# The low parts of five weight tiles computed on GpSimd instead of VectorE, in a hybrid decoder layer on one core

## The chip, the cores and the metric

One core of a Trainium2 chip runs the whole kernel. The metric is the time of one execution on the device, in microseconds (us); smaller is better. Engines are named as the profile names them: PE (TensorE), ACT (ScalarE), DVE (VectorE), POOL (GpSimd), SP (SyncE, which here only issues DMAs).

## The reference, cut to what matters

One decoder layer on 512 positions of width 1024: a mixer of three parallel branches, cross-attention to 256 memory rows, and a gated MLP. The change lies in the mixer, whose input product `h @ w_in` feeds every branch:

```python
xa, ga, q, k, v, z, beta_raw, alpha_raw, uc, gates = jnp.split(h @ w_in, offs, axis=-1)
ya = rg_lru(causal_dwconv(xa, a_conv_w) + a_conv_b, a_w_r, a_b_r, a_w_i, a_b_i, a_lam) * jax.nn.gelu(ga)
...
o = chunk_gated_delta_rule(q, k, v, g, beta)
...
yc = jax.nn.gelu(s5_layer(uc, c_lam_re, c_lam_im, c_log_dt, c_b_re, c_b_im, c_c_re, c_c_im, c_d))
yc = (yc * jax.nn.sigmoid(yc @ c_glu_w.astype(f32) + c_glu_b.astype(f32))).astype(h.dtype)
branches = jnp.stack([ya, yb, yc], axis=2)
proj = jnp.einsum('bskc,kcd->bskd', branches, w_branch)
gate = jax.nn.sigmoid((gates + b_gate).reshape(bsz, s, N_BRANCH, D_MODEL))
return jnp.sum(gate * proj, axis=2) @ w_out
```

`rg_lru` takes two sigmoids of small block products of `xa`, forms `a = exp(log_a)` and `b = sqrt(1 - a*a) * ig * x`, and runs the recurrence `h = a*h + b` along the sequence. `s5_layer` runs a complex recurrence with 64 states in each of 32 groups.

## The kernel before, in words

**Weights.** All weights come as 179 tiles of 128 x 1024 (512 KB), in the order of the list `ORDER` (L40). Each product is float32 made of three passes of a rounded form: a weight tile `raw` is loaded by SP (`w_dma`, L207), ACT copies it rounded into `whi` (`w_split`, L222, by `act` at L145), and `wlo = raw - whi` is one `tensor_tensor` of 128 x 1024 (L223, by `tt` at L148; on DVE). PE then multiplies, for each of 8 slabs of 128 rows, `whi` by the high part of the activations, `whi` by their low part, and `wlo` by their high part (`passes`, L235): 24 products of 128 x 512 for a tile, the third of which is the first to read `wlo`. The names in the profile are `hh` and `hl` for the activations' two parts, `ps_in` and `ps_gate` for the results.

**Buffers.** `raw`, `whi` and `wlo` have three buffers each (`WB` = 3), so `whi` of tile n is written into the buffer of tile n-3, and waits until PE has done with that tile. `wnext` (L227) splits two tiles ahead.

**The stretch around the change.** Tiles 17 to 30 in `ORDER` are: 17 `("in", XA)`, 18 `("in", GA)`, 19 and 20 the second pair of `XA`, `GA`, 21 to 24 the four `Z_` tiles, 25 to 28 the last two pairs of `XA`, `GA`, 29 to 32 `gate` tiles of the first branch, and after these `("br", 0, 0)`, the first branch's products. Beside these products run three generators, each of which hands out its small work a piece at a time between the weight products: `rglru` (L900, four calls: PE makes `pr` and `pi` from `xfga`, ACT takes tanh, exp and a square root, DVE the `MEMSET` of one column at L921, the scan at L924 and the split into `yah` and `yal`), the gated delta rule (transposes `trp` on PE, whose squares ACT sums into `ss` through `junk`), and `s5` (L1085). In `s5`, ACT copies `ks` from the products `pk` (L1171), SP writes it to DRAM as `kd` with eight DMAs (L1176), and eight DMAs on ACT's queue read it back into `T` (L1194), which POOL has cleared before (L815). DVE meanwhile forms `F` from `fa`, `fb`, turns `rot` by two doublings (`s5_double`, L1068), and then does four rounds of a rotation into `Wd`, two scans `ra` (L1215) and a rotation back; for each round POOL makes a small tensor `D` (a `MEMSET` of 128 x 4 and one operation of 128 x 252). POOL's other work ahead of it is the polynomial of the gates' exponentials (`ge`, `gr`, from L822) and the first doublings of `rot` (L809).

**Order.** The program is written in the order of the generators, but the framework's scheduler (`schedule_with_timeline_sim=True`) sorts each engine's instructions by a simulated timeline; an engine then runs its own list strictly in that order, and its DMA queue likewise.

Of the kernel before, what the change touches and what calls it, by code (L numbers as in the profile page):

```python
# [10 lines left out]
ALU = mybir.AluOpType  # L11
# [25 lines left out]
XA, GA, Q_, K_, V_, Z_ = 0, 4, 8, 12, 16, 20  # L37


def weight_order():  # L40
    o = [("uc", t) for t in range(4)]
    for b in (K_, Q_, V_):
        o += [("in", b + t) for t in range(4)]
        if b == Q_:
            o.insert(-3, ("ba",))
    for t in range(4):
        o += [("in", XA + t), ("in", GA + t)]
        if t == 1:
            o += [("in", Z_ + t) for t in range(4)]
    for br in (0, 2, 1):  # L50
        gt = lambda mp: [("gate", br * 8 + 2 * mp), ("gate", br * 8 + 2 * mp + 1)]
        ahead = GA_N[br]
        first = [k for mp in range(ahead) for k in gt(mp)]
        if br == 1:
            for m in range(2):
                o += [("wk", 4 * m + i) for i in range(4)] + [("gate", br * 8 + m)]
            for c in range(2):
                o += [("wv", c, kp) for kp in range(4)] + [("gate", br * 8 + 2 + c)]
        else:
            o += first  # L60
        if br == 2:
            o += [("glu", 0), ("glu", 1)]
        for mp in range(4):
            o += (gt(mp) if mp >= ahead else []) + [("br", br, mp)]
    o += [("out", m) for m in range(8)]
    o += [("wq", m) for m in range(8)]
    o += [("wo", m) for m in range(8)]
    for half in range(2):
        for i in range(12 * half, 12 * half + 12):
            o += [("up", i), ("up", 24 + i)]  # L70
        if half == 0:
            o += [("down", c, kp) for c in range(2) for kp in range(6)]
        else:
            o += [("dn9", t) for t in range(9)] + [("dn3", t) for t in range(3)]
    return o


ORDER = weight_order()


class Layout:
# [20 lines left out]
class Kern:  # L102
# [104 lines left out]
    def w_dma(self, upto):  # L207
        while self.dma_i < min(upto, len(ORDER)):
            i = self.dma_i
            t = self.raw.tile([128, 1024], F32, tag="raw", name=f"raw{i}")  # L210
            self.nc.sync.dma_start(out=t, in_=self.ap["wts"][i])
            self.rawt[i] = t
            self.dma_i += 1

    def w_split(self, upto):
        while self.split_i < min(upto, len(ORDER)):
            i = self.split_i
            self.w_dma(i + 1)
            r = self.rawt.pop(i)
            h = self.whi.tile([128, 1024], F32R, tag="hi", name=f"whi{i}")  # L220
            l = self.wlo.tile([128, 1024], F32R, tag="lo", name=f"wlo{i}")
            self.act(h, r)  # L222
            self.tt(l, r, h, ALU.subtract)  # L223
            self.wt[i] = (h, l)
            self.split_i += 1

    def wnext(self, key, ahead=WB - 1):  # L227
        i = self.wi
        assert ORDER[i] == key, (ORDER[i], key)
        self.wi += 1  # L230
# [577 lines left out]
    def gt(self, out, a, b, op):  # L808
        return self.pin(self.nc.gpsimd.tensor_tensor(out=out, in0=a, in1=b, op=op))  # L809
# [745 lines left out]
def tiles_of(inputs):  # L1555
# [6 lines left out]

    out = np.empty((len(ORDER), 128, 1024), np.float32)
    for i, key in enumerate(ORDER):
        t, o = key[0], out[i]
# [119 lines left out]
```

## Time and profile before

| what | value |
|---|---|
| median of three runs | 1071.02 us (1071.0 to 1071.41) |
| the profiled execution | 1071.09 us |
| its span in the profile | 1069.2 us |
| granted TensorE clock, mean | 0.998 of full speed |
| PE busy | 1050.0 us, 98% of the span |
| DVE busy | 700.9 us, 66% |
| ACT busy | 502.7 us, 47% |
| POOL busy | 148.8 us, 14% |

The span runs from the first recorded instruction to the last; the 1.9 us between it and the execution's time lie outside the records. Times within the span are counted from its start. Shares are means over stages that are limited by different things, so a stage is read by its own rows.

### The profile page before, as it was taken

The page shows a single profiled execution, that of the slowest core. Times are in us where ns is not written, and L with a number is a line of the kernel's source. Part 1 is how long each engine was busy: PE and PEld are TensorE (multiplying, and loading weights), DVE is VectorE, ACT ScalarE, POOL GpSimd, SP SyncE. Part 2 cuts the span into 40 slices and gives each one's busy share as a digit, 9 for nine tenths or more (in the row PEclk, how much of TensorE's full clock was granted, in tenths as well). Part 3 has the DMA queues.
Part 4 walks back from the last instruction along what each step waited for, and adds up shares of the span by engine and source line. Part 5 has one row for each costly group of instructions (what it writes and reads, how often), then busy time and mean ns, then how long its engine had stood idle before and what let it go on. Part 6 is the DMA issues. An engine that isn't in the chain of part 4 may idle for free.

```text
span 1069.2 us, 13413 instructions
## 1 busy us (share of the span) xinstructions
PE 1050.0 (98%) x5098; PEld 873.9 (82%) x5098; DVE 700.9 (66%) x1024; ACT 502.7 (47%) x808; POOL 148.8 (14%) x285
## 2 busy tenths in 40 slices
PE   8999999999999999999999999999999999999996
PEld 6878878788877898888888878888888888888885
DVE  6798589958899554755545456577763357777423
ACT  6566766658244444633444344544442124444313
POOL 6899822000000100000000000000000000000004
PEclk9999999999999999999999999999999999999999
DMA  8362232255324431432422114222223233222222
GB/s 288 118 158 80 67 100 79 80 126 189 109 79 148 109 100 64 145 125 96 145 100 95 59 37 139 81 99 99 80 98 99 99 99 99 99 98 91 91 75 79
DMA packets 45168, 112.81 MB, mean 106 GB/s; under 512 B 10656, under 2 KB 16432, under 8 KB 44848
## 3 DMA queue, kind: packets, MB, share of 16 engines
q1 hardware_dynamic: 41088, 108.52, 31.7%
q10 hardware_dynamic: 3760, 3.18, 1.0%
q0 software_dynamic: 256, 0.26, 0.3%
q8 instruction: 40, 0.66, 0.3%
q14 instruction: 24, 0.20, 0.1%
HBM read 107.08 MB, written 4.86 MB: 105 GB/s over the span
## 4 chain that ended last, share of the span: by engine, by line
PE 67%; DVE 13%; POOL 12%; issue 3%; ACT 2%; DMA 1%; SPq 0%; POOLq 0%; ACTq 0%; DVEq 0%
PE ps_up L160 24%; PE psdn L160 11%; PE ps_gate L160 6%; PE ps_wq L160 4%; PE ps_out L160 4%; PE ps_wo L160 4%; POOL s5p L809 3%; PE psb L160 3%; DVE wlo L148 2%; PE ps_wk L160 2%; PE psv L160 2%; POOL s5P L153 2%; DVE nBX L148 1%; POOL s5p L154 1%; PE sc L160 1%
## 5 line engine op out<-in xcount | busy, mean ns | idle before, releaser
L148 DVE TENSOR_TENSOR wlo<-raw,whi 128x1024 fp32r<-128x1024 f32 (+1 forms) x185 | 220.2, 1194 | 168.8 <-ACT whi L145 163.8
L145 ACT ACTIVATE whi<-raw 128x1024 fp32r<-128x1024 f32 (+1 forms) x185 | 189.9, 1030 | 285.2 <-PE psdn L160 84.1
L160 PE MATMUL ps_up<-xgh,whi 128*128 128x512 f32 x384 | 150.2, 391 | 0.0
L160 PE MATMUL ps_up<-xgh,wlo 128*128 128x512 f32 x384 | 150.0, 391 | 0.0
L160 PE MATMUL ps_up<-xgl,whi 128*128 128x512 f32 x384 | 149.5, 389 | 0.0
L148 POOL TENSOR_TENSOR y<-xt,gfin 128x512 f32<-128x512 f32 x4 | 5.4, 1343 | 688.9 <-DVE xt L148 688.9
L160 PEld LDWEIGHTS ps_up<-xgh,wlo 128*128 128x128 f32 x384 | 72.1, 188 | 15.4 <-issue 0.2
L160 PEld LDWEIGHTS ps_up<-xgh,whi 128*128 128x128 f32 x384 | 72.1, 188 | 14.9 <-issue 0.2
L160 PEld LDWEIGHTS ps_up<-xgl,whi 128*128 128x128 f32 x384 | 72.1, 188 | 14.7
L160 PE MATMUL ps_gate<-hh,whi 128*128 128x512 f32 x192 | 75.6, 394 | 1.5 <-DVE pr L157 1.5
L160 PE MATMUL ps_gate<-hh,wlo 128*128 128x512 f32 x192 | 75.4, 393 | 0.0
L160 PE MATMUL ps_gate<-hl,whi 128*128 128x512 f32 x192 | 75.1, 391 | 0.0
L160 PE MATMUL psdn<-wlo,acth 128*128 128x512 f32 x192 | 74.4, 389 | 0.0
L160 PE MATMUL psdn<-whi,actl 128*128 128x512 f32 x192 | 74.4, 389 | 0.0
L160 PE MATMUL psdn<-whi,acth 128*128 128x512 f32 x192 | 73.9, 389 | 0.0
L157 DVE SCALAR_TENSOR_TENSOR fu<-pad,par,fu 128x512 f32<-128x512 f32 x96 | 71.5, 749 | 1.8 <-ACT fu L145 0.3
L160 PE MATMUL ps_in<-hh,whi 128*128 128x512 f32 x168 | 67.8, 403 | 0.0
L160 PE MATMUL ps_in<-hh,wlo 128*128 128x512 f32 x168 | 65.8, 392 | 0.1
L160 PE MATMUL ps_in<-hl,whi 128*128 128x512 f32 x168 | 65.7, 391 | 0.0
L148 DVE TENSOR_TENSOR pad<-ps_up,rb 128x512 f32<-128x512 f32 x48 | 32.9, 688 | 44.8 <-PE ps_up L160 43.5
L145 ACT ACT_TABLE_LOAD x32 | 41.1, 1283 | 18.8 <-DVE yp L157 10.1
L160 PEld LDWEIGHTS ps_gate<-hh,whi 128*128 128x128 f32 x192 | 36.1, 188 | 9.3 <-DVE pr L157 1.9
(394 smaller groups left out, 2181.8 us busy)
## 6 DMA issues: line engine op xcount, KB each, us to landing
raw<-wts SPq DMA_DIRECT2D x177, 512.0 KB, 3.4
x<-xT SPq DMA_DIRECT2D x14, 256.0 KB, 4.2
raw<-wts SPq DMA_DIRECT2D x8, 128.0 KB, 4.8
BC<-bc SPq DMA_DIRECT2D x1, 1024.0 KB, 8.2
ud<-uperm SPq DMA_DIRECT2D x4, 256.0 KB, 3.2
U<-ud SPq DMA_DIRECT2D x8, 128.0 KB, 6.2
uu<-ud SPq DMA_DIRECT2D x4, 256.0 KB, 3.4
yd<-T SPq DMA_DIRECT2D x8, 128.0 KB, 3.2
```

The lines of the kernel that those rows point to most:

```text
L145: return self.nc.scalar.activation(out=out, in_=in_, func=func, **k)
L148: return (eng or self.nc.vector).tensor_tensor(out=out, in0=a, in1=b, op=op)
L153: return e.tensor_scalar(out=out, in0=a, scalar1=s1, scalar2=None, op0=op0)
L154: return e.tensor_scalar(out=out, in0=a, scalar1=s1, scalar2=s2, op0=op0, op1=op1)
L157: return self.nc.vector.scalar_tensor_tensor(out=out, in0=a, scalar=s, in1=b, op0=op0, op1=op1)
L160: return self.nc.tensor.matmul(out, lhsT=lhsT, rhs=rhs, start=start, stop=stop)
L809: return self.pin(self.nc.gpsimd.tensor_tensor(out=out, in0=a, in1=b, op=op))
```

## The change

A constant names every third weight tile from tile 18 to the tile ahead of `("br", 0, 0)`, and the subtraction that makes `wlo` of these tiles is given to POOL. Tiles 18, 21, 24, 27 and 30 are the ones named; the other 174 stay on DVE.

```diff
 ORDER = weight_order()
 
+POOL_LO = range(ORDER.index(("in", GA)), ORDER.index(("br", 0, 0)), 3)
+
...
             h = self.whi.tile([128, 1024], F32R, tag="hi", name=f"whi{i}")
             l = self.wlo.tile([128, 1024], F32R, tag="lo", name=f"wlo{i}")
             self.act(h, r)
-            self.tt(l, r, h, ALU.subtract)
+            self.tt(l, r, h, ALU.subtract, self.nc.gpsimd if i in POOL_LO else None)
             self.wt[i] = (h, l)
             self.split_i += 1
```

The scheduler's order is another on all engines between tile 18 and about tile 35, and the same elsewhere. Line numbers of the changed kernel are higher by 2. In the rows that follow, the digits right behind `whi`, `wlo` and `raw` are the weight tile's number, and the digits behind the underscore only count tensors.

ACT, from the rounding of tile 20 to `T`, before:

```order
L145 ACTIVATE whi20_1413<-raw20_1264 128x1024
L145 ACTIVATE vraw_462<-cv_1201 128x512
L145 ACTIVATE pad0_118<-ps_in_1259 128x512
L145 ACTIVATE junk_1313,ss_1281<-trp_1302 128x128 x4
...
L145 ACT_TABLE_LOAD
L145 ACTIVATE xfga_1258<-ps_in_1412 128x512
L145 ACTIVATE whi21_1469<-raw21_1417 128x1024
...
L145 ACT_TABLE_LOAD
...
L145 ACTIVATE ks_1499<-pk5_1354 128x512
...
L1194 DMA T_1497<-kd5_1353 16x16x64
...
L145 ACTIVATE whi22_1538<-raw22_1473 128x1024
```

and after the change:

```order
L147 ACTIVATE whi20_1413<-raw20_1264 128x1024
L147 ACTIVATE whi21_1469<-raw21_1417 128x1024
L147 ACTIVATE vraw_462<-cv_1201 128x512
L147 ACTIVATE pad0_118<-ps_in_1259 128x512
L147 ACT_TABLE_LOAD
L147 ACTIVATE xfga_1258<-ps_in_1412 128x512
...
L147 ACTIVATE xfga_1258<-pad0_118,par_84 128x512
L147 ACTIVATE whi22_1538<-raw22_1473 128x1024
L147 ACTIVATE pad1_120<-ps_in_1468 128x512
...
L147 ACTIVATE xfga_1258<-pad1_120,par_84 128x512
...
L147 ACT_TABLE_LOAD
...
L147 ACTIVATE ks_1499<-pk5_1354 128x512
```

The rounding of tile 21 moved up from behind the two groups of `junk` and the table load to right behind tile 20's, and the rounding of tile 22, `pad1` and an `xfga` moved up from behind `ks` and the first DMA of `T` to ahead of `ks`; one table load more stands ahead of `ks` (three instead of two).

DVE, around the subtraction of tile 29 in the third and fourth rounds of `s5`, before:

```order
L148 TENSOR_TENSOR rg0_1712<-rg0_1712,xfga_1258 128x512
L148 TENSOR_TENSOR rb5_1893<-rot_1170,Wd_880 128x512
L148 TENSOR_TENSOR ha_1988<-s5P_123,Wd_880 128x8x63
L148 TENSOR_TENSOR wlo29_1910<-raw29_1868,whi29_1909 128x1024
L157 SCALAR_TENSOR_TENSOR xfga_1258<-pad0_118,par_84,xfga_1258 128x512
L148 TENSOR_TENSOR hb_1989<-s5P_123,Wd_880 128x8x63
L1215 SCALAR_TENSOR_TENSOR ra_1835<-D5_1837,Wd_880 128x256 x2
L148 TENSOR_TENSOR Wd_880<-ra_1892,rb5_1893 128x256 x2
```

and after the change:

```order
L150 TENSOR_TENSOR rg0_1712<-rg0_1712,xfga_1258 128x512
L150 TENSOR_TENSOR rb5_1893<-rot_1170,Wd_880 128x512
L150 TENSOR_TENSOR ha_1988<-s5P_123,Wd_880 128x8x63
L150 TENSOR_TENSOR hb_1989<-s5P_123,Wd_880 128x8x63
L1217 SCALAR_TENSOR_TENSOR ra_1835<-D5_1837,Wd_880 128x256 x2
L159 SCALAR_TENSOR_TENSOR xfga_1258<-pad0_118,par_84,xfga_1258 128x512
L150 TENSOR_TENSOR wlo29_1910<-raw29_1868,whi29_1909 128x1024
L150 TENSOR_TENSOR Wd_880<-ra_1892,rb5_1893 128x256 x2
L150 TENSOR_TENSOR yal0_1257<-rg0_1712,yah0_1256 128x512
```

`hb`, two scans `ra` and an `xfga` moved from behind `wlo29` to ahead of it; in the stretch from the first `MEMSET rg` to `wlo29`, `wlo27` is gone from DVE.

POOL, from the clearing of `T` on, before:

```order
L815 MEMSET T_1497 128x2048
L815 MEMSET D5_1694 128x4
L153 TENSOR_SCALAR D5_1694<-s5P_123 128x4x63
L815 MEMSET D5_1765 128x4
L153 TENSOR_SCALAR D5_1765<-s5P_123 128x4x63
L815 MEMSET D5_1837 128x4
L153 TENSOR_SCALAR D5_1837<-s5P_123 128x4x63
L815 MEMSET D5_1894 128x4
L153 TENSOR_SCALAR D5_1894<-s5P_123 128x4x63
L815 MEMSET H0_1986 128x4
L815 MEMSET H1_1987 128x4
```

and after the change:

```order
L811 TENSOR_TENSOR rot_1170<-k1_1175,k2_1176 128x16x8
L150 TENSOR_TENSOR wlo24_1659<-raw24_1602,whi24_1658 128x1024
L817 MEMSET D5_1694 128x4
L155 TENSOR_SCALAR D5_1694<-s5P_123 128x4x63
L817 MEMSET D5_1765 128x4
L155 TENSOR_SCALAR D5_1765<-s5P_123 128x4x63
L150 TENSOR_TENSOR wlo27_1818<-raw27_1781,whi27_1817 128x1024
L817 MEMSET D5_1837 128x4
L155 TENSOR_SCALAR D5_1837<-s5P_123 128x4x63
L817 MEMSET D5_1894 128x4
L155 TENSOR_SCALAR D5_1894<-s5P_123 128x4x63
L150 TENSOR_TENSOR wlo30_1952<-raw30_1913,whi30_1951 128x1024
L817 MEMSET H0_1986 128x4
```

Subtractions of tiles 24, 27 and 30 stand in POOL's list ahead of, between and behind the four `D` of `s5`; those of tiles 18 and 21 stand further up, among the polynomial and the first doublings.

## Rows read from the trace of the kernel before

**Rows 1.** The page, part 1: busy time, share of the span, instructions.

```profile
PE 1050.0 (98%) x5098; PEld 873.9 (82%) x5098; DVE 700.9 (66%) x1024; ACT 502.7 (47%) x808; POOL 148.8 (14%) x285
```

**Rows 2.** Windows: busy time of PE, PEld, DVE, ACT, POOL; granted clock, DMA share, GB/s.

```profile
150.00:200.00 50.00, 48.66 (x206) 38.37 (x206) 48.63 (x82) 34.59 (x45) 8.14 (x11) 1.00 0.27 87
```

**Rows 3.** Groups by form: busy us, mean ns | idle before. One of DVE, one of POOL.

```profile
L148 DVE TENSOR_TENSOR wlo<-raw,whi 128x1024 fp32r<-128x1024 f32 x177 | 216.8, 1228 | 167.9 <-ACT whi L145 163.0 <-PE rbp L160 3.9
...
L148 POOL TENSOR_TENSOR y<-xt,gfin 128x512 f32<-128x512 f32 x4 | 5.4, 1343 | 688.9 <-DVE xt L148 688.9
```

**Rows 4.** Timeline of ACT, 118 to 158 us: start, us, line, operation [idle <-releaser].

```profile
118.17 1.06 ACT L145 ACTIVATE whi<-raw 128x1024 fp32r<-128x1024 f32 x1 [1.50 <-PE ps_in L160]
120.04 0.63 ACT L145 ACTIVATE vraw<-cv 128x512 f32<-128x512 f32 x1 [0.81 <-DVE cv L157]
...
122.24 0.28 ACT L145 ACTIVATE junk<-trp 128x128 f32<-128x128 f32 x1 [1.08 <-PE trp L163]
...
129.51 1.05 ACT L145 ACTIVATE whi<-raw 128x1024 fp32r<-128x1024 f32 x1
...
133.13 1.28 ACT L145 ACT_TABLE_LOAD   x1
...
134.66 0.58 ACT L145 ACTIVATE ks<-pk 128x512 f32<-128x512 f32 x1
...
140.14 0.65 ACTq L1194 DMA_DIRECT2D T<-kd  x1
...
140.94 1.06 ACT L145 ACTIVATE whi<-raw 128x1024 fp32r<-128x1024 f32 x1
...
142.54 0.80 ACT L145 ACTIVATE xfga<-pad,par 128x512 f32<-128x512 f32 x1
...
157.31 0.63 ACT L145 ACTIVATE rg<-rg 128x512 f32<-128x512 f32 x1
```

**Rows 5.** Timeline of PE, first products of weight tile 18.

```profile
118.20 0.39 PE L160 MATMUL ps_in<-hh,whi 128*128 128x512 f32 x1
118.42 0.39 PE L160 MATMUL ps_in<-hl,whi 128*128 128x512 f32 x1
```

**Rows 6.** Timeline of SyncE's queue; then the landing of these DMAs.

```profile
135.26 5.21 SPq L1176 DMA_DIRECT2D kd<-ks  x8
...
DMA to landing us min/median/max: 2.0/2.0/2.1
```

**Rows 7.** Timeline of POOL: clearing of T, the last of three.

```profile
138.31 1.80 POOL L815 MEMSET T<- 128x2048 f32 x1
```

**Rows 8.** Windows: busy time of DVE, 158.00 to 189.58 us.

```profile
158.00:189.58 31.58, 31.48 (x55) 1.00 0.25 86
```

**Rows 9.** Timeline of DVE, 158 to 193 us.

```profile
158.00 0.06 DVE L921 MEMSET rg<- 128x1 f32 x1
...
189.58 1.21 DVE L148 TENSOR_TENSOR wlo<-raw,whi 128x1024 fp32r<-128x1024 f32 x1
190.72 0.74 DVE L157 SCALAR_TENSOR_TENSOR xfga<-pad,par,xfga 128x512 f32<-128x512 f32 x1
191.38 0.67 DVE L148 TENSOR_TENSOR hb<-s5P,Wd 128x504 f32<-128x504 f32 x1
191.97 1.26 DVE L1215 TENSOR_TENSOR_SCAN ra<-D,Wd 128x256 f32<-128x256 f32 x2
```

**Rows 10.** Timeline of PE: the third product of weight tile 29, and pr.

```profile
190.85 0.50 PE L160 MATMUL ps_gate<-hh,wlo 128*128 128x512 f32 x1
...
195.21 1.12 PE L160 MATMUL pr<-xfga,wg 128*128 128x512 f32 x2 [1.34 <-DVE xfga L157]
```

**Rows 11.** Timelines of POOL and DVE: two operations at the same time.

```profile
154.89 1.24 POOL L153 TENSOR_SCALAR D<-s5P 128x252 f32<-128x252 f32 x1
...
155.35 1.41 DVE L148 TENSOR_TENSOR wlo<-raw,whi 128x1024 fp32r<-128x1024 f32 x1
```

**Rows 12.** Timeline of DVE beside the clearings of POOL.

```profile
135.17 4.97 DVE L153 TENSOR_SCALAR rq<-ss 128x16 f32<-128x16 f32 x1
```


## The prediction

> **What bounds the kernel now.** I read the page first: PE is busy 98% of the span [rows 1], so a change elsewhere costs time only where PE is made to wait, and gains time only where PE waits today. Then the windows of 50 us around the change: in 150 to 200 us PE is busy 48.66 us [rows 2], and the 1.34 us that lack are one wait, of `pr` for DVE's `xfga` [rows 10]. That is all that the five subtractions taken from DVE could give back. Then DVE in the same stretch: between the first `MEMSET rg` and `wlo29` it works 31.48 of 31.58 us [rows 8], and `wlo29` ends at 190.79, just when PE's first product with it starts, 190.85 [rows 9, 10]. DVE has no slack there; a microsecond lost to DVE ahead of tile 29 is lost to PE, but for what the order behind it gives back. Last, the chain that sets the beginning of that stretch, followed back from `MEMSET rg`: it waits for ACT's square root (157.31), which stands in ACT's list behind the DMAs of `T` (from 140.14), which wait for `kd`, which SP writes once ACT has made `ks` (ends 135.24); and ACT worked without a pause from 122.24 to `ks` [rows 4, 6].
>
> **The change, part by part.** The sum is made against the profiled execution, 1071.09 us, 0.07 above the median shown.
>
> *The subtractions themselves.* DVE loses five of 1.23 us [rows 3], issued 1.14 apart, POOL gains five. POOL took 1.34 us for half as many elements with two inputs [rows 3], so I estimate 2.4 to 2.7 us each. A tile is split two tiles ahead of its use, some 10 us (2 x 24 x 0.225 [rows 5]), four times as long as that, so for tiles 18, 21, 24 and 30 I cost it at nothing: PE's products of the two tiles between hide it. If that cover went, each would cost PE at most the difference of the durations, 1.2 to 1.5 us. `wlo27` stands behind two `D` in POOL's list, and is about in time.
>
> *ACT's order.* The rounding of tile 21 now stands directly behind tile 20's. It needs the buffer of tile 18, and PE begins tile 18 at 118.20 and takes 24 products at 0.22 to 0.23 us each [rows 5]: the buffer is free at 123.6. ACT has ended tile 20 at 119.2 [rows 4], and now stands still for 4.4 us with everything behind it: `vraw`, `pad`, all of the `junk`, `ks`. From 123.6 on it has to do what it did between 122.24 and 135.24, starting 1.36 later; `vraw` and `pad`, done until now by 121.16, 1.1; the rounding of tile 22, `pad` and `xfga` that stood behind the first DMA of `T` (140.94 to 143.34, 2.25 of it work ahead of `ks` now, since the ends overlap); and a third table load, 1.28 [rows 4]. `ks` ends at 135.24 + 1.36 + 1.1 + 2.25 + 1.28 = 141.2.
>
> *SP and ACT's queue.* Half of `kd`, four DMAs at 0.65, and a landing of 2.0 us [rows 6] lie between `ks` and the first DMA of `T`: the fourth is issued by 143.8 and lands at about 145.5. Until now that first DMA went at 140.14, released by POOL's clearing of `T` (ends 140.11 [rows 7]). POOL clears `T` later too, by a subtraction (2.4) less a few small operations, about 142.3: no longer what is last. So `T` starts +5.4. From there to the square root it was 17.2 us [rows 4]; that stretch gets one table load and loses the three operations that moved up, which I put at -0.3. `MEMSET rg` comes 5.1 later, at 163.1.
>
> *DVE's order.* From `MEMSET rg` to `wlo29`, `wlo27` is gone (-1.14), and `hb`, two scans and an `xfga` have come (0.59 + 1.2 + 0.66 = 2.45 [rows 9]): 31.6 + 1.3 = 32.9. `wlo29` starts at 196.0 and ends at 197.2, 6.4 later than now. PE, whose own products I take to have slipped by under 1 us by then (the later roundings ahead of it), waits in tile 29 at its third product. Behind `wlo29` DVE has five operations of 0.6 to 0.66 to the `xfga` that `pr` needs, 3.2 us: `pr` at 200.4, where it was 195.21 with its wait in it. **+5.2 us**, and PE has no slack behind it to win that back. The earlier waits (tiles 25 to 28) are parts of this, not added.
>
> *DVE and POOL at the same time.* No row shows a subtraction on POOL beside dense DVE work. Tiles 27 and 30 fall there (24 before it). Bounds: nothing, if they run side by side. Nearest row: `D` on POOL, 252 columns and 1.24 us, beside a DVE subtraction of 1.41 instead of 1.23 [rows 11, 3], 0.18 lost. Scaled by columns read (2048 for 252) this is 1.5 us for a subtraction, by POOL's time (2.4 for 1.24) 0.4. Far row: a DVE operation of 16 columns that began at 135.17 ended at 140.14, when POOL's clearings ended [rows 12, 7]: whole standstill, 2.4 each. I take 0.9 each, between the two scalings because `D` is the row that also reads: **+1.8 us** (0 to 4.8). A gain is excluded, DVE being full.
>
> The Trainium skill ("SBUF — State Buffer", section "Who interferes with whom") says that a VectorE instruction with two SBUF inputs contends with a GpSimd instruction that reads SBUF, and that the one which comes second is blocked for the whole of the first. By that the term would be 4.8 instead of 1.8, and the sum 1081.1; the `D` rows speak for less, the clearings for as much.
>
> Sum: 1071.1 + 5.2 + 1.8 = **1078.1 us**. Without contention 1076.3.
>
> **The rivals.**
>
> *Not slower, 1071.3.* ACT's standstill is absorbed. The DVE order alone costs 1.3 and gives back 1.1 (`pr` follows `wlo29` after 3.2 us, not 4.4), so the time is unchanged as long as `MEMSET rg` comes less than about a microsecond later; from there each microsecond counts in full. For it: PE slips little before tile 25, so tile 18's buffer comes when said; the `junk` waited for PE's transposes at 122.24 anyway, 1.08 us [rows 4]; and if ACT's chain between `T` and the square root holds waits that shrink (17.2 us, in part the issue of DMAs), much of the 5.1 vanishes. Against it: the 13 us of ACT before `ks` have no pause, and `ks` to `T` to the root is in list order. 0.21.
>
> *Whole standstill, 1081.1.* As the rule above has it; decided by whether a DVE operation beside POOL's `wlo27` and `wlo30` grows by over 2 us. 0.15.
>
> *Faster, 1069.8.* DVE is relieved, nothing else is late, and the 1.34 wait goes. This is still within 0.2% of now (2.1 us, about what a measurement of this kernel can tell from no change); over that would need time from outside the stretch, where the order is the same. 0.04 for it.
>
> That the change doesn't do what it says: the range could have named none or many tiles; the order shows five subtractions on POOL, so I leave this out.
>
> **How the numbers follow.** The forecast, with contention between nothing and most of a standstill (1073.3 to 1080), has 0.60; the whole standstill 0.15; not slower 0.21; faster 0.04. The likeliest gives 1078.1. Slower by over 0.2%: 0.60 + 0.15 = 0.75; within: 0.21; faster: 0.04. The range: down to 1071.0, the rival without a cost, leaving out the faster tail and the lower part of that rival (about 0.10); up to 1082.0, the standstill with a microsecond of slip (about 0.09 beyond). The likeliest case's own range is 1075.5 to 1080.5.
>
> **What would show it.** In the profile after: ACT idle from 119 to 123.6 ahead of a `whi`, released by PE; `ks` ending near 141; the first `T` near 145.5; `MEMSET rg` near 163; `wlo29` starting near 196; PE waiting five us or so in all for DVE between 165 and 205, where it waits 1.34 now, most of it in `ps_gate` for `wlo`. POOL's five `wlo` at 2.4 to 2.7 us. DVE's operations beside `wlo27` and `wlo30` longer by about 0.9 in all for each. Wrong it would be if `MEMSET rg` stays at 159 or earlier (first rival), if POOL's subtractions take four us or more because DVE starves them, so that PE waits for POOL instead, or if DVE's operations stand still for the whole of one.

## The result and the profile after

| | before | after |
|---|---|---|
| median | 1071.01 us (1070.9 to 1071.41, 4 runs) | 1078.3 us (1078.28 to 1078.4, 4 runs) |
| span of the profiled execution | 1069.2 us | 1076.5 us |
| granted TensorE clock, mean | 0.998 | 0.994 |

The change makes the kernel slower by 7.3 us: the ratio is 1.0062 (95% interval 1.005 to 1.0074). The forecast was 1078.1. That the number came out does not yet say that its terms did; two of them were off, one by over one and one by over two microseconds, in opposite directions.

The page's first part and the windows of the two stretches after (columns as in [rows 1] and [rows 2]):

```profile
PE 1053.3 (98%) x5098; PEld 876.1 (81%) x5098; DVE 697.9 (65%) x1019; ACT 505.5 (47%) x810; POOL 164.1 (15%) x290
```

```profile
150.00:200.00 50.00, 45.56 (x186) 36.43 (x185) 43.60 (x73) 35.74 (x46) 15.42 (x11) 0.93 0.25 77
200.00:250.00 50.00, 48.41 (x253) 39.91 (x252) 35.01 (x54) 27.45 (x44) 3.45 (x10) 1.00 0.45 122
```

DVE is busy 3.0 us less than before and POOL 15.3 us more: five subtractions have moved. PE, which lacked 1.34 us in 150 to 200 us [rows 2], now lacks 4.44 there and 1.59 in the next window, and has a granted clock of 0.93 in the first. The waits of PE name the two (us in total, times, longest):

```profile
PE ps_in L162 <- DVE wlo L150: 4.4, 1, 4.4
...
PE pr L162 <- DVE xfga L159: 1.6, 1, 1.6
```

Where they come from is read back from `pr`. DVE's timeline:

```profile
161.49 0.06 DVE L923 MEMSET rg<- 128x1 f32 x1
...
176.20 3.42 DVE L1217 TENSOR_TENSOR_SCAN ra<-D,Wd 128x256 f32<-128x256 f32 x2
...
188.98 1.21 DVE L150 TENSOR_TENSOR wlo<-raw,whi 128x1024 fp32r<-128x1024 f32 x1
...
196.34 1.21 DVE L150 TENSOR_TENSOR wlo<-raw,whi 128x1024 fp32r<-128x1024 f32 x1
...
199.95 2.86 DVE L159 SCALAR_TENSOR_TENSOR xfga<-pad,par,xfga 128x512 f32<-128x512 f32 x1
```

Against [rows 9]: `MEMSET rg` comes at 161.49 instead of 158.00, 3.49 later. Between it and the `xfga` that `pr` needs (ends 202.81) two operations stand out. Two scans `ra`, 1.26 us in [rows 9], take 3.42; an `xfga`, 0.74, takes 2.86. These are 2.16 and 2.12 us of standstill. POOL's timeline has a subtraction at each of the two places:

```profile
132.88 2.36 POOL L150 TENSOR_TENSOR wlo<-raw,whi 128x1024 fp32r<-128x1024 f32 x1
...
157.65 2.40 POOL L150 TENSOR_TENSOR wlo<-raw,whi 128x1024 fp32r<-128x1024 f32 x1 [12.67 <-ACT whi L147]
...
176.20 2.87 POOL L150 TENSOR_TENSOR wlo<-raw,whi 128x1024 fp32r<-128x1024 f32 x1 [6.11 <-ACT whi L147]
...
195.81 6.44 POOL L150 TENSOR_TENSOR wlo<-raw,whi 128x1024 fp32r<-128x1024 f32 x1 [9.17 <-DVE ra L1217]
```

These are tiles 21, 24, 27 and 30; tile 18's stands ahead of this stretch. Tiles 21 and 24 met no dense DVE work and took 2.36 and 2.40 us. Tile 27 began with the scans and ran 2.87. Tile 30 began at 195.81 and ended at 202.25. By the 2.4 us of the others it stood some 4 us while DVE went on, and then DVE stood while it ran. So `pr` is late by 3.49 + 2.16 + 2.12, less 0.1 for the changed list of DVE: 7.65 us (202.86 against 195.21 [rows 10]). At the end of the span 7.3 are left; a wait of 0.5 us that `pq` had on DVE's `nA` before is gone.

The 3.49 us at `MEMSET rg` are ACT's, whose timeline answers to [rows 4]:

```profile
117.72 1.06 ACT L147 ACTIVATE whi<-raw 128x1024 fp32r<-128x1024 f32 x1 [1.51 <-PE ps_in L162]
123.21 1.06 ACT L147 ACTIVATE whi<-raw 128x1024 fp32r<-128x1024 f32 x1 [4.43 <-PE ps_in L162]
...
140.17 0.58 ACT L147 ACTIVATE ks<-pk 128x512 f32<-128x512 f32 x1
...
145.06 0.65 ACTq L1196 DMA_DIRECT2D T<-kd  x1
...
147.71 1.28 ACT L147 ACT_TABLE_LOAD   x1 [0.97 <-issue]
...
160.80 0.63 ACT L147 ACTIVATE rg<-rg 128x512 f32<-128x512 f32 x1
```

The second rounding waited 4.43 us for PE to end tile 18; `ks` ended at 140.75, and `T`'s first DMA went at 145.06, 5.51 and 4.92 later than before, in an execution that was 0.45 us ahead of the other when tile 20's rounding began (117.72 against 118.17). Counted from that rounding, `T` comes 5.37 later, `MEMSET rg` 3.94 and `pr` 8.10.

PE's timeline at its longest wait shows one thing more:

```profile
185.42 0.39 PE L162 MATMUL ps_in<-hl,whi 128*128 128x512 f32 x1
190.25 0.80 PE L162 MATMUL ps_in<-hh,wlo 128*128 128x512 f32 x1 [4.44 <-DVE wlo L150]
190.84 0.63 PE L162 MATMUL ps_in<-hh,whi 128*128 128x512 f32 x1
...
202.86 1.13 PE L162 MATMUL pr<-xfga,wg 128*128 128x512 f32 x2 [1.59 <-DVE xfga L159]
```

```profile
190.00:192.00 2.00, 1.75 (x4) 1.46 (x5) 2.00 (x6) 1.10 (x3) 0.00 (x0) 0.50 0.37 90
...
194.00:196.00 2.00, 2.00 (x7) 1.52 (x6) 2.00 (x4) 2.00 (x4) 0.19 (x1) 0.50 0.00 0
...
198.00:200.00 2.00, 2.00 (x11) 1.65 (x10) 2.00 (x5) 1.55 (x2) 2.00 (x1) 1.00 0.69 211
```

After the 4.44 us the granted clock is 0.50 (the lower of TensorE's two levels, 1.2 instead of 2.4 GHz) until 196 us, and products start 0.43 us apart instead of 0.23. Some 13 products cost 2.6 us more. In this execution this sets nothing: PE reaches `pr` and still waits 1.59 us for DVE, so at full clock it would only have waited longer there. In the second profile of the change, below, a low clock falls behind `pr` as well, and there it does cost time.

### The profile page after: what moved, and what is told of

Its sections match the earlier page's. It is cut to its first block, busy times and chain, and to the rows that moved or that the text cites. A ratio compares the mean times of both kernels' runs of the same rounds, so it can differ in the third digit from the quotient of the medians.

```text
span 1076.5 us, 13408 instructions
## 1 busy us (share of the span) xinstructions
PE 1053.3 (98%) x5098; PEld 876.1 (81%) x5098; DVE 697.9 (65%) x1019; ACT 505.5 (47%) x810; POOL 164.1 (15%) x290
## 4 chain that ended last, share of the span: by engine, by line
PE 84%; DVE 8%; ACT 2%; issue 2%; DMA 1%; POOL 1%; SPq 0%; ACTq 0%; POOLq 0%; DVEq 0%
PE ps_up L162 24%; PE psdn L162 11%; PE ps_gate L162 10%; PE ps_in L162 7%; PE psb L162 5%; PE ps_wq L162 4%; PE ps_out L162 4%; PE ps_wo L162 4%; PE ps_uc L162 2%; PE ps_wk L162 2%; PE psv L162 2%; PE pv L162 2%; DVE nBX L150 1%; DVE wlo L150 1%; PE sc L162 1%
## 5 line engine op out<-in xcount | busy, mean ns | idle before, releaser
L150 DVE TENSOR_TENSOR wlo<-raw,whi 128x1024 fp32r<-128x1024 f32 (+1 forms) x180 | 214.0, 1193 | 168.4 <-ACT whi L147 163.6
```

The lines of the kernel that those rows point to most:

```text
L150: return (eng or self.nc.vector).tensor_tensor(out=out, in0=a, in1=b, op=op)
```

## The experiments

The theory after this profile: two costs that add up, each with its own tiles. Tile 18 on POOL sets off the changed list of ACT, which makes `MEMSET rg` late; tiles 27 and 30 each stop DVE for 2.1 us. Rivals: the order alone, or the standstill alone, is the cause, and the other is covered. All experiments but the last change only which engine makes which low part, or add an operation on POOL that nobody waits for; the last one moves a clearing of POOL. Each ratio is against the kernel before on the same chip; its median there was 1071.45 in the first four runs, 1071.88 in the next, 1072.09 in the last.

| tiles on POOL | median, us | ratio to before (95% interval) | `MEMSET rg` | `pr` |
|---|---|---|---|---|
| none (the profile before) | 1071.01 | 1 | 158.00 | 195.21 |
| 18 | 1076.27 | 1.0042 (1.0029 to 1.0055) | 162.18 | 199.26 |
| 21 | 1076.43 | 1.0048 (1.0035 to 1.006) | 164.08 | 201.27 |
| 27, 30 | 1075.67 | 1.0039 (1.0025 to 1.0053) | 157.85 | 200.08 |
| 21, 24, 27, 30 | 1080.41 | 1.0079 (1.0066 to 1.0091) | 162.54 | 203.87 |
| 18, 21, 24 | 1075.91 | 1.0033 (1.0021 to 1.0045) | 161.81 | 198.78 |
| 24, 27, 30 | 1075.62 | 1.0034 (1.0023 to 1.0045) | 158.12 | 199.46 |
| 18, 21, 24, 27, 30 (the change, again) | 1078.71 | 1.0063 (1.0051 to 1.0075) | 162.89 | 204.22 |

The last two columns count from the start of the span, and the profiled executions do not all reach the stretch at the same time: tile 20's rounding begins between 117.72 and 119.08 us (118.17 in the kernel before). Counted from that rounding, `MEMSET rg` is 3.94 to 3.98 us later than before in all four profiles with tile 18 on POOL (the change, the change again, 18 alone, and 18, 21 and 24). `pr` is 8.10 later in both profiles of the change, 3.84 with tile 18 alone, 3.73 with 18, 21 and 24, 5.59 with tile 21 alone, 4.98 with 27 and 30, 9.02 with 21, 24, 27 and 30, and 4.36 with 24, 27 and 30. Behind `pr` the executions differ by up to some two microseconds that are only in part traced back here, so the rows up to `pr` say more about a step than the total times do.

**Tile 18 alone.**

```diff
-POOL_LO = range(ORDER.index(("in", GA)), ORDER.index(("br", 0, 0)), 3)
+POOL_LO = (18,)
```

> Only tile 18 on POOL; ACT's list is the changed kernel's up to T (tile 21's rounding right behind tile 20's), DVE's list around tiles 25 to 29 is that of the kernel before, and no subtraction of POOL stands beside DVE's dense stretch. Theory (two separate costs: the list order set off by tile 18, and a standstill of DVE during each of tiles 27 and 30): MEMSET rg some 3.5 us later than before (161.5 instead of 158.0), pr 3.5 later, no DVE operation stretched, time 1074.5 (1073.5 to 1075). Rival 1 (the standstills are all of it, ACT's order is absorbed): 1071.0. Rival 2 (the order is all of it, and the stretched operations only replace PE waits that would be there anyway): 1078.

Measured: 1.0042, 4.8 us where 3.5 were expected; `MEMSET rg` at 162.18, no operation of DVE stretched, `pr` 4.05 later. ACT's second rounding waits as in the change:

```profile
123.87 1.06 ACT L147 ACTIVATE whi<-raw 128x1024 fp32r<-128x1024 f32 x1 [4.43 <-PE ps_in L162]
```

The time lies above the expected range (up to 1075); the later run of tiles 18, 21 and 24 gives 3.8. But both rivals fall: one subtraction, moved to where POOL had time for it, costs about half of the whole at `pr`. That this goes through the list and not through the subtraction's own duration is read from this row, where ACT waits for PE and not for POOL; no run keeps the changed lists with all subtractions on DVE.

**Tiles 27 and 30 alone** (the same line with `(27, 30)`).

> Only tiles 27 and 30 on POOL; ACT's list up to T is that of the kernel before. DVE's work between MEMSET rg and the xfga that pr waits for is that of before less one subtraction plus two operations of 0.6, +0.06. Theory: MEMSET rg at 158.0, one DVE operation stretched by 2.1 us beside each of POOL's two subtractions, pr 4.3 later, time 1075.3 (1074.3 to 1076). If DVE is only slowed as I had put it before, 0.9 each: 1072.9. Rival 1 (standstills are all of it): 1078. Rival 2 (order is all): 1071.

Measured: 1.0039, `MEMSET rg` where it was, and a stretched pair of scans beside each subtraction (3.42 and 3.37 instead of 1.26). The 0.9 each of the prediction falls, 2.1 each stands, and the time is in the expected range. Tile 18 alone and this run add up to 9.0 us, more than the 7.3 of the change; each is known to about 1.4 us, so this sum alone does not settle that the costs add up. The two halves below do better.

**The change without tile 18** (`(21, 24, 27, 30)`).

> The change less tile 18: tiles 21, 24, 27 and 30 on POOL, ACT's list up to T as before. Theory: the same as tiles 27 and 30 alone, since 21 and 24 fall where DVE has idle time: 1075.3 (1074.3 to 1076), ACT not idle from 119 to 123. If tile 18's place in the order were nothing: 1078.3 as with the change.

Measured: 1080.41, where 1075.3 was expected. Here the theory failed: taking away the tile whose list change costs four microseconds gained nothing. The ratio, 1.0079, is above the change's 1.0063, but the two intervals overlap, so slower still it is not shown to be. `MEMSET rg` came at 162.54 although ACT did not stand still; the next run shows why.

**Tile 21 alone** (`(21,)`).

> Only tile 21 on POOL: the lists of all other engines are those of the kernel before, less that one subtraction on DVE. Theory: within 0.1% of before, 1070.9 to 1071.5, POOL's clearing of T (ends 140.1 before) up to 2.4 us later, which would move T's first DMA by as much and pr by up to 2.4 us unless kd's landing is what T waits for: so 1071.0 if kd is last, up to 1073.4 if the clearing is. Rival (any subtraction on POOL beside other work costs what it does on tiles 27 and 30): 1073.

Measured: 1.0048, five microseconds for a move that leaves every other engine's list as it was. `T`'s first DMA went at 145.30, and not because of the clearing. The timeline of SyncE's queue, and POOL's around tile 21, in this run:

```profile
121.64 19.28 SPq L213 DMA_DIRECT2D raw<-wts  x2
140.98 5.22 SPq L1178 DMA_DIRECT2D kd<-ks  x8
```

```profile
134.64 3.56 POOL L817 MEMSET F<- 128x2048 f32 x2
138.17 2.39 POOL L150 TENSOR_TENSOR wlo<-raw,whi 128x1024 fp32r<-128x1024 f32 x1
140.50 1.81 POOL L817 MEMSET T<- 128x2048 f32 x1
```

POOL's list has tile 21 behind the two clearings of `F`, so `raw` of tile 21 is read until 140.56 (138.17 + 2.39); before, DVE had read it by 131.8. The load of tile 24 needs that buffer, and stands in SP's list ahead of the eight DMAs of `kd`: they begin at 140.98, although `ks` was there at 135.69. I had costed tile 21 at nothing, with PE's products as its cover; its buffer has another claimant. In the change itself this is hidden: there tile 21 stands ahead of `T`'s clearing and is done at 135.24, before `ks` (140.75). In the run without tile 18 it was not: there `kd` began at 140.15 with `ks` ready at 134.86.

**Only the hold on the buffer.** To test that reading, all subtractions stay on DVE, and POOL only reads four columns of that tile:

```diff
+        self.scr = self.cpool.tile([128, 4], F32, name="scr")
...
+            if i == 21:
+                self.tt(self.scr, r[:, 0:4], h[:, 0:4], ALU.subtract, self.nc.gpsimd)
```

> The kernel before with one POOL operation more: 4 columns of raw21 less whi21 into a scrap tile, behind the two clearings of F; all subtractions on DVE, all other lists unchanged. It leaves POOL's time as it is (about 0.2 us) and only holds raw21's buffer until about 138.5 instead of 131.8. Theory (with tile 21 alone on POOL, the load of tile 24 waits for raw21's buffer at the head of SP's list, and the eight DMAs of kd stand behind it): kd's first DMA at 138.8 instead of 135.3, T's first at about 143, MEMSET rg and pr 2.5 to 3.5 us later, time 1073.7 to 1074.7. Rival (what costs there is POOL's 2.4 us, through the later clearing of T or a standstill of DVE): 1071.4, as before.

```profile
121.11 17.65 SPq L214 DMA_DIRECT2D raw<-wts  x2
138.82 5.23 SPq L1181 DMA_DIRECT2D kd<-ks  x8
```

`kd` from 138.82, `T` from 143.01, `MEMSET rg` at 160.87 and `pr` at 198.08: each as expected. The time is 1073.38, 1.0016 (1.0007 to 1.0025), 1.5 us and not 2.3 to 3.3; of the 2.87 us at `pr` the trace has 2.2 left behind `pq`, whose wait of 0.5 us is gone, and 1.8 at the end. An operation of four columns costs this kernel 1.5 us because of where it stands.

**What in POOL's operation stops DVE.** Three kernels with the lists of before and one more operation on POOL for tiles 27 and 30, into a scrap tile: two inputs, one, none.

```diff
+        self.scr = self.cpool.tile([128, 1024], mybir.dt.bfloat16, name="scr")
...
+            if i in (27, 30):
+                self.tt(self.scr, r, h, ALU.subtract, self.nc.gpsimd)
```

> The kernel before with two POOL operations more: raw less whi of tiles 27 and 30, 128 x 1024, into a scrap tile (bf16) that nobody reads; DVE makes all low parts itself and all other lists are unchanged. Theory (a POOL subtraction stops DVE's two-input operations for nearly its whole duration): one DVE operation of some 3.4 instead of 1.26 or 2.8 instead of 0.7 beside each; pr 2.1 later if only tile 27's falls ahead of it, 4.3 if both do; time 1073.5 to 1075.7. Rival (what cost time with tiles 27 and 30 is the changed order of DVE's list, the stretched operations being waits): 1071.4.

```diff
+                self.ts(self.scr, h, 1.0, eng=self.nc.gpsimd)
```

> As the run with two inputs, but POOL only copies whi of tiles 27 and 30 into the scrap tile (one input, times 1.0). If any POOL operation that reads stops DVE for its whole duration: DVE operations stretched by that duration (1.5 to 3 us each by the 1.56 us of 128 x 512 with one input), time 1074 to 1076. If a stop goes with the second input: no stretched operation over 0.2 us, time 1071.4 to 1071.8.

```diff
+                self.pin(self.ts(self.scr[:, 0:4], h[:, 0:4], 1.0, eng=self.nc.gpsimd))
+                self.pin(self.nc.gpsimd.memset(self.scr, 0.0))
```

> As the run with two inputs, but POOL only clears the scrap tile, behind a copy of 4 columns of whi that holds it in its place. If an operation that only writes stops DVE's two-input operations too (a DVE operation of 16 columns stood still beside POOL's clearings in the kernel before): stretched operations and over 1072.5. If not: 1071.4, no DVE operation stretched by over 0.2 us.

POOL's timeline and DVE's beside it, two inputs:

```profile
172.09 3.48 POOL L151 TENSOR_TENSOR scr<-raw,whi 128x1024 bf16<-128x1024 f32 x1 [4.92 <-ACT whi L148]
...
192.12 2.89 POOL L151 TENSOR_TENSOR scr<-raw,whi 128x1024 bf16<-128x1024 f32 x1 [7.85 <-ACT whi L148]
```

```profile
172.69 3.42 DVE L1220 TENSOR_TENSOR_SCAN ra<-D,Wd 128x256 f32<-128x256 f32 x2
...
192.68 2.88 DVE L160 SCALAR_TENSOR_TENSOR xfga<-pad,par,xfga 128x512 f32<-128x512 f32 x1
```

One input:

```profile
172.48 3.85 POOL L156 TENSOR_SCALAR scr<-whi 128x1024 bf16<-128x1024 f32 x1 [4.92 <-ACT whi L148]
...
191.13 3.27 POOL L156 TENSOR_SCALAR scr<-whi 128x1024 bf16<-128x1024 f32 x1 [7.85 <-ACT whi L148]
```

```profile
173.08 2.06 DVE L1220 TENSOR_TENSOR_SCAN ra<-D,Wd 128x256 f32<-128x256 f32 x2
...
191.69 1.52 DVE L160 SCALAR_TENSOR_TENSOR xfga<-pad,par,xfga 128x512 f32<-128x512 f32 x1
```

None:

```profile
173.95 0.95 POOL L229 MEMSET scr<- 128x1024 bf16 x1
...
191.19 0.95 POOL L229 MEMSET scr<- 128x1024 bf16 x1
```

```profile
173.19 1.26 DVE L1221 TENSOR_TENSOR_SCAN ra<-D,Wd 128x256 f32<-128x256 f32 x2
...
190.97 0.73 DVE L160 SCALAR_TENSOR_TENSOR xfga<-pad,par,xfga 128x512 f32<-128x512 f32 x1
```

The same two groups of DVE, a pair of scans and an `xfga`, take 3.42 and 2.88 us beside two inputs, 2.06 and 1.52 beside one, 1.26 and 0.73 beside none: 2.15 lost each, 0.8 each, nothing. The times are 1.0047 (1.0034 to 1.0059), 1.0015 (1.0006 to 1.0024) and 1.0001 (0.9992 to 1.001). In the first, DVE's list is that of before, so the rival that blamed the list falls; at 1076.44 it lies a little above the expected 1075.7, with `pr` 4.12 later as expected. The second lies between its two expectations: a POOL operation that reads one tensor stops DVE too, but for 0.8 of the 3.3 to 3.9 us that it lasts, not for the whole. Between these two runs the kind of operation changes with the number of inputs (a subtraction, a multiplication by 1.0); no run parts the two.

**The change once more, and its two halves.**

> The changed kernel once more, beside the other runs of this group on the same chip, as their measure. Theory: 1.006 to 1.007 of before; MEMSET rg at 161.5 to 162.2, two DVE operations stretched by 2.1 us each.

> Tiles 18, 21 and 24 on POOL, 27 and 30 back on DVE. Theory (the lists' order through tile 18, whose delay of ks covers tile 21's hold on SP's list, is one part; the stops beside tiles 27 and 30 are the other): MEMSET rg at 161.5 to 162.2 as in the change, pr 3.5 to 4.2 later than before, no DVE operation between MEMSET rg and pr stretched by over 0.3 us; time of before + 3.5 to 4.8. If tiles 18 and 21 added up as their single runs would (4.0 and 6.0 us at MEMSET rg): over + 8.

> Tiles 24, 27 and 30 on POOL, 18 and 21 back on DVE. Theory: MEMSET rg at 158.0 as before, two DVE operations stretched by 2.1 us, time of before + 4.3, as with 27 and 30 alone; if tile 24's subtraction meets DVE's work ahead of MEMSET rg as well, up to 2 us more.

In one group of runs on one chip: 1075.91 for tiles 18, 21 and 24, 1075.62 for 24, 27 and 30, 1078.71 for all five, against 1072.09: 3.8 + 3.5 = 7.3 beside 6.6 measured, and by the intervals the same. At `pr`, counted from tile 20's rounding, it is 3.73 + 4.36 = 8.09 beside 8.10. The halves add up, and tile 21's hold is covered by tile 18's delay, as said. With tiles 24, 27 and 30, tile 24 did stretch one operation ahead of `MEMSET rg` (2.74 instead of 0.69); DVE had idle time behind it, and `MEMSET rg` came 0.1 later (158.12). The change again had `MEMSET rg` at 162.89, outside the 161.5 to 162.2 expected: that execution was late before the stretch began (tile 20's rounding at 119.08), and counted from there it is the same 3.98. It was also the slowest of its six (1080.94): behind `pr`'s wait of 2.42 us the granted clock fell once more, to 0.50 between 206 and 208 us, where PE has no wait to hide it in. From `pr` to the next wait, at `psb`, this execution took 1.3 us longer than the first profile of the change (123.18 against 121.88), which fits that.

**A way to gain on the kernel before.** All of this goes through the chain `kd`, `T`, square root, `MEMSET rg`. In the kernel before, `T`'s first DMA waited for the clearing of `T` [rows 4, 7], not for `kd`:

```diff
         F = [self.slot("F0"), self.slot("F1")]
-        for t in F:
+        T = self.slot("T")
+        for t in (T, *F):
             self.gz(t, 0.0)
...
-        T = self.slot("T")
-        self.gz(T, 0.0)
```

> The kernel before with T cleared ahead of the two F instead of behind them, all subtractions on DVE; DVE's and SP's lists are unchanged. Theory (the chain kd, T, square root, MEMSET rg sets pr): T's first DMA goes when kd has landed, at 139.2 to 139.4, not when the clearing ends at 140.1; MEMSET rg and pr 0.8 us earlier, the wait for pr 0.5 instead of 1.34, time of before less 0.8 (0.08%, below what the measurement can tell; the trace tells it). If something else sets MEMSET rg: T earlier, MEMSET rg still at 158.0.

```profile
139.18 0.65 ACTq L1195 DMA_DIRECT2D T<-kd  x1
```

`T` goes at 139.18, `MEMSET rg` at 157.06, `pr` at 194.28, each 0.9 earlier. Of that, 0.37 is this execution's head start (tile 20's rounding at 117.80); the move itself gives 0.6, less than the 0.8 expected, and PE's wait for `pr` is 0.96 and not 0.5. The 0.6 is what `kd` allows: `T` follows 4.31 us behind the first `kd` here, as it does in the runs above where `kd` is last (4.2 to 4.3), and followed it by 4.88 before. The time is 1070.99 against 1072.09, 0.9993 (0.9984 to 1.0001): the direction is as expected, and the measurement cannot tell it from no change. No version here beats the kernel before by more than that.

## Why the prediction was right, and where it was not

- *What bounds the kernel*: right. At `pr` all the loss is set by DVE's chain from `MEMSET rg` on, and the chain behind `MEMSET rg` is the one named (`ks`, `kd`, `T`, square root).
- *Subtractions of 2.4 to 2.7 us on POOL*: right where DVE leaves POOL alone (2.36 to 2.40). That the other tiles cost nothing was right of this change only: tile 21 alone costs 5 us, through the buffer it holds and SP's list, which my step did not look at.
- *ACT's order*: right. Idle 4.43 (4.4 forecast), `ks` at 140.75 (141.2; the execution was 0.45 ahead), `T`'s clearing to 142.19 (142.3), `T`'s first DMA at 145.06 (145.5); counted from tile 20's rounding, `T` is 5.37 later, forecast 5.4.
- *From `T` to the square root*: **mis-sized**. I put the change of that stretch at -0.3; it went from 17.17 to 15.74 us, -1.43. The row that I did not use is the idle time of ACT ahead of the next table load, put down to issue:

```profile
145.79 1.28 ACT L145 ACT_TABLE_LOAD   x1 [2.46 <-issue]
```

  2.46 us before, 0.97 after (147.71 above): before, all eight DMAs of `T` stood in ACT's list ahead of that load, after only four do. The 0.97 stands in all four profiles with tile 18 on POOL. So `MEMSET rg` came at 161.49, not 163.1: 1.1 of the difference is this term, 0.45 the execution's head start.
- *DVE's order*: right in size (together with the operations behind `wlo29` it nets to nothing), but not in place. The long wait is in tile 28's third product, not in tile 29's, because `wlo28` went down DVE's list as well and a standstill lies ahead of it: it began 24.3 us behind `MEMSET rg` before, 27.5 after (188.98), of which the standstill of the scans is 2.16. Before:

```profile
182.32 1.21 DVE L148 TENSOR_TENSOR wlo<-raw,whi 128x1024 fp32r<-128x1024 f32 x1
```

- *DVE and POOL at the same time*: **this step failed**. I took 0.9 us each from the `D` row [rows 11]; the runs show 2.15 each, 4.3 instead of 1.8. `D` has one input and a subtraction has two, and the runs with one and two inputs differ by just that (0.8 and 2.15): scaled from 252 to 1024 columns, the 0.18 of `D` are 0.73, which is what one input cost, and it was no measure of a subtraction. The far row, the clearings [rows 12], was nearer in its result, though a clearing does nothing to DVE's two-input operations (the run without inputs). The rival of the whole standstill had the mechanism and got 0.15: its sign, a DVE operation beside each subtraction longer by over 2 us, is what the profile shows (2.16 and 2.12). Another sign of being wrong came in part, a subtraction of over four microseconds on POOL (tile 30, 6.44), but PE did not wait for it. The sentence of the Trainium skill beside it ("SBUF — State Buffer", section "Who interferes with whom") agrees with the trace for two inputs (2.15 us lost, of 2.36 to 2.40 that a subtraction takes) and for none; for one input the blocking was 0.8 of 3.3 to 3.9 us, less than the whole, and there the measurement decides.
- *The sum*: 5.2 + 1.8 = 7.0 forecast at `pr` and taken for the end, 3.5 + 4.2 = 7.65 measured at `pr`, 7.3 at the end. The number was right by luck, because -1.6 at `MEMSET rg` (1.1 of it the term above) and +2.4 beside POOL nearly cancelled. Of the other rivals, *not slower* is excluded by tile 18 alone, and *faster* by every run that moves a subtraction.

## What to carry to other kernels

Where a scheduler orders the instructions, moving one operation to an idle engine can cost more by the new order than by itself: compare the lists, and for each operation that moved up ask which buffer it waits for and what stands behind it. For an operation that goes to a slower engine, follow its input's buffer to the next load and to everything behind that load in the same queue. And before work goes to GpSimd beside dense VectorE work, count its inputs: here two cost VectorE nearly the operation's whole duration, one about a quarter of it, none nothing.

## What the runs showed of the hardware that I had not expected

- How much a POOL operation stopped DVE's two-input operations went with its inputs: 128 x 1024 with two inputs 2.15 us, with one 0.8, a clearing 0.
- It goes the other way as well: POOL's subtraction of tile 30 stood some 4 us (6.44 instead of 2.4) while DVE worked through several operations without a gap. The trace before had a sign of it, the third `D` beside dense work of DVE, 2.91 us where the others took 1.16 to 1.24:

```profile
174.39 2.91 POOL L153 TENSOR_SCALAR D<-s5P 128x252 f32<-128x252 f32 x1
```

- After a PE wait of 4.44 us the granted clock was 0.50 for about 6 us. With tile 18 alone, three waits of 1.0 to 1.5 us between 180 and 200 us left it at 1.00; with tiles 18, 21 and 24, two of 1.48 and 1.77 us went with a mean of 0.83 between 190 and 200 us; beside one input on POOL, a wait of 2.10 us left it at 1.00. What decides between these, no run here tells.
